# Two-layer hybrid trunk: in the RWKV pairs, the value mix behind the 16x16 inverse, the bonus sum in the eighth PSUM bank, the removal-query transposes behind the key-query products

## The chip, the cores and the metric

The kernel runs on one core of one Trainium2 chip. The metric is the device time of one execution, in microseconds (us). A core has a matrix engine (TensorE, PE in the profile; its weight loads are PEld), a vector engine (VectorE, DVE), an activation engine (ScalarE, ACT), GpSimd (POOL) and SyncE (SP). Here nearly all transfers are issued from SP's queue, in the order of the program. Matrix products are written to PSUM, which has eight banks of 128x512 fp32; this kernel gives them out as four kinds of buffer: `bank` (tag a, two), `bank2` (tag b, two), `gbank` (tag g, three) and `bank3` (tag h, one, "the eighth bank").

## The reference, cut to what matters

Each of the two layers normalises x (512 tokens, 2048 features), multiplies it with a wide input matrix, runs three branches (mLSTM, latent attention, RWKV-7), gates and joins their outputs and multiplies with an output matrix. The branch that the change touches:

```python
def rwkv7_branch(rw_mix, v_first, vres, mu, w0, w2, a0, a2, k_k, k_a, r_k, ln_g, ln_b):
    xm = rw_mix.astype(jnp.float32)
    xs = xm + mu * (token_shift(xm) - xm)
    r, k, v, xw, xa = jnp.split(xs, [...], axis=-1)
    decay = jnp.exp(-jnp.exp(-jax.nn.softplus(-(w0 + jnp.tanh(xw) @ w2)) - 0.5))
    a = jax.nn.sigmoid(a0 + xa @ a2)
    if vres is None:                      # layer 0
        v_first = v
    else:                                 # layer 1: the value mix
        v0, v1, v2 = vres
        v = v + (v_first - v) * jax.nn.sigmoid(v0 + (v @ v1) @ v2)
    kk = heads(k * k_k)                   # 8 heads of 64
    kk = kk / jnp.maximum(jnp.sqrt(jnp.sum(kk * kk, axis=-1, keepdims=True)), 1e-12)
    k_h = heads(k * (1.0 + (a - 1.0) * k_a))
    y = rwkv7_scan(heads(r), heads(decay), k_h, heads(v), -kk, kk * heads(a))
    y = head_layer_norm(y, ...)           # then the bonus:
    y = y + jnp.sum(heads(r) * k_h * r_k, axis=-1, keepdims=True) * heads(v)
    return y.reshape(B, T, RW_WIDTH), v_first
```

The scan is S = S*w + (S a) b^T + v k^T, y = S r, over 512 tokens. `a_vec` = -kk is the removal query, `b_vec` = kk*a the removal key.

## The kernel before, in words

Matrix products with full precision are done in three passes: an operand is split in a rounded part and a rest (`hi`, `lo`), ACT makes the first and DVE the second (L150, L151 for weights; L252, L254 in `split2`).

Per layer, the input product is cut in 26 blocks of 256 columns. `gemm` (L221) makes a generator of 8 steps for each block; each step is 12 matmuls of 128x512 (24 of 128x256 for `mv`) in PSUM tiles called `pg0_..` and `pg1_..`. The weights come in pieces of 512 KB (`raw_..`) from SP's queue, two buffers deep. The generators stand in one list, `bg`. The foreground work, which has long chains of small operations, calls for them: `bg.along(ratio, main, side)` runs a foreground generator and takes `ratio` background steps for each of its `yield`s; `bg.ensure(name)` runs background steps until the block `name` is done. So where the code yields, and where it needs a block, sets how much of the input product is written beside which foreground work. From that order of the code a list scheduler with a timing model (`schedule_with_timeline_sim=True`) makes a fixed order for each engine when the program is built; on the chip each engine takes its instructions in that order. Inside `with in_order():` PE's order is as written.

The foreground of a layer, in order: four pairs of RWKV heads (`rw_pair`, L694, ratio 1.0); then `rw_states` beside the mLSTM heads 0 and 1 (`ml_head`, ratio 0.8); then three short preparations of the attention beside the mLSTM heads 2 and 3; then `bg.ensure("az3")`, the last of the input product; then the attention (`attention`, ratio 0.0), and the output product (`po`, L1390).

A pair works on two heads, that is 128 features by 512 tokens, in 8 chunks of 64 tokens. Its chain: decays `E`, `Ei` and gate `al`; keys `k` and their norm (`psn`, a product with block ones that sums over a head); `ar` holds the removal queries and the queries, `bk` the two kinds of keys (four POOL instructions, L785); the bonus sum (`psbo`, `head_sum` at L760) is copied to `bv`; the values `v` are fetched, in layer 1 mixed with layer 0's (L767 to L776: a product `psv2`, a sigmoid, three DVE instructions and a fetch of `vf`), multiplied into the bonus and parked; values and removal queries are transposed to token-major form (`psTv` to `UV`, `psTa` to `AR`; `token_major`, L790). Then the key-query products of each chunk (`psG`, 16 matmuls in two `bank` and two `bank2` tiles) go masked to `GG` (L822), and the keys are transposed (`psTk`). The 16x16 diagonal blocks go through DRAM (`inv_d`) to a layout in which DVE inverts them in a loop of short instructions (`TX`, L879 to L890), and back (`tx`); two doublings to 64x64 follow (`psQ`, `psT32`, `psQ64`, `psX64`). `psQ` stands in one in-order stretch with `psR` (L919), the first product that reads `UV`. The products with the inverse (`psW`, `psM`, `psN`, `psY`) end the pair.

`fetch("rv")` (L764) asks for the block `rv0` or `rv1` of the values, and in layer 1 line 766 asks for `rv1` in any case, so in the first pair of a layer the code there runs all background steps up to that block.

Of the kernel before, what the change touches and what calls it, by code (L numbers as in the profile page):

```python
# [12 lines left out]
F32 = mybir.dt.float32  # L13
# [4 lines left out]
ALU = mybir.AluOpType  # L18
# [40 lines left out]
R_MU, R_W0, R_A0, R_KK, R_KA, R_RK, R_LG, R_LB, R_V0 = 66, 79, 83, 87, 91, 95, 99, 103, 107  # L59
# [14 lines left out]
def trunk(ctx, tc, a, out):  # L74
    nc = tc.nc
    mm = nc.tensor.matmul
# [3 lines left out]
    tt = nc.vector.tensor_tensor  # L80
    dma = nc.sync.dma_start

    def in_order():

        return tc.manual_schedule(engines={mybir.EngineType.PE})
# [10 lines left out]
    def bank(name):  # L96
        return psb.tile([128, 512], F32, tag="a", bufs=2, name=name)
# [121 lines left out]
    bg = Work()  # L219
# [31 lines left out]
    def split2(hi, lo, src, scale=1.0):  # L251
        act(hi, src, AF.Copy, scale=scale)  # L252
        if isinstance(scale, float) and scale == 1.0:
            tt(lo, src, hi.bitcast(F32), ALU.subtract)  # L254
        else:
            stt(lo, src, scale, hi.bitcast(F32), ALU.mult, ALU.subtract)

    def sigm(dst, src, hbias):

        act(dst, src, AF.Tanh, scale=0.5, bias=hbias)  # L260
        tsc(dst, dst, 0.5, 0.5, ALU.mult, ALU.add)
# [112 lines left out]
    ps = bank("psng")  # L374
# [140 lines left out]
    vf_d = dram.tile([4, 128, T], F32, name="vf_d")  # L515

    for l in range(DEPTH):
        bg.done.clear()

        def pc(r, l=l):  # L520
            return prm[l][:, r:r + 1]

        def pch(r, l=l):
            return prh[l][:, r:r + 1]
# [8 lines left out]
        kept = {}  # L533
# [137 lines left out]
        tail_d = dram.tile([4, 3, 128, T], F32, name=f"tail_d{l}")  # L671
        xp = xp_ctx.enter_context(tc.tile_pool(name=f"xp{l}", bufs=1, side="left"))
        rp = rp_ctx.enter_context(tc.tile_pool(name=f"rp{l}", bufs=1, side="right"))
# [9 lines left out]
        if l > 0:  # L683
            v1 = rp.tile([128, 4, 32], F32, name=f"v1_{l}")
            nc.gpsimd.dma_start(v1, a["rw_v1"][l - 1].rearrange("(k p) r -> p k r", p=128))
            raw = rp.tile([32, T], F32, tag="UV", name=f"v2r_{l}")
            nc.gpsimd.dma_start(raw, a["rw_v2"][l - 1])
            v2 = rp.tile([128, T], F32R, name=f"v2_{l}")
# [5 lines left out]
        def rw_pair(p, l=l):  # L694
            nm = f"{l}_{p}"

            def tmp(name):
                return rp.tile([128, T], F32, tag="tmp", bufs=4, name=f"{name}{nm}")
            whh, ahh, wl, al_ = kept["wa"]

            def fetch(kind):
                bg.ensure(f"{kind}{p // 2}")
                t = rp.tile([128, T], F32, tag=f"x{kind}", name=f"x{kind}{nm}")
                dma(t, vf_d[p] if kind == "rv" and l == 0 else park_d[PARK[kind] + p])
                return t
            inv_d = inv_ds[p]

            def head_sum(x, tag, name):

                hl = rp.tile([128, 2, T], F32R, tag=tag, name=f"{name}x{nm}")  # L710
                split2(hl[:, 0], hl[:, 1], x)
                ps = bank(f"{name}{nm}")
                for u in range(2):
                    mm(ps, lhsT=bones, rhs=hl[:, u], start=(u == 0), stop=(u == 1))
                return ps
            sl = slice(p * 128, (p + 1) * 128)

            ps = bank(f"psw{nm}")
# [6 lines left out]
            s = tmp("s")  # L725
# [14 lines left out]
            act(inv, k, AF.Square, scale=pc(R_KK + p))  # L740
            ps = head_sum(inv, "UV", "psn")
            yield
# [6 lines left out]
            ar = rp.tile([128, 2, 8, 64], F32, tag="ar", name=f"ar{nm}")  # L749
# [7 lines left out]
            tt(kk, kk, al, ALU.mult)  # L757
            bo = tmp("bo")
            stt(bo, r, pc(R_RK + p), kh, ALU.mult, ALU.mult)
            ps = head_sum(bo, "AR", "psbo")  # L760
            yield
            bv = tmp("bv")
            nc.scalar.copy(bv, ps)
            v = fetch("rv")  # L764
            if l > 0:
                bg.ensure("rv1")
                ps = bank(f"psv2_{nm}")  # L767
                mm(ps, lhsT=v2[:, p * 128:(p + 1) * 128], rhs=kept["vv"], start=True, stop=True)
                yield
                s = tmp("vs")  # L770
                sigm(s, ps, pch(R_V0 + p))
                vf = tmp("vf")
                dma(vf, vf_d[p])
                tt(vf, vf, v, ALU.subtract)
                tt(vf, vf, s, ALU.mult)
                tt(v, v, vf, ALU.add)  # L776
            tt(bv, bv, v, ALU.mult)
            dma(tail_d[p, 0], bv)

            hs = [slice(0, 64), slice(64, 128)]  # L780
            bk = rp.tile([128, 8, 2, 64], F32, tag="bk", name=f"bk{nm}")
# [8 lines left out]
            def token_major(blocks, dst, nn, bank_=bank):  # L790

                ps = bank_(f"psT{nn}{nm}")
                for tb in range(4):
                    nc.tensor.transpose(ps[:, tb * 128:(tb + 1) * 128], blocks(tb), idf)
                pv = ps.rearrange("p (a n) -> p a n", n=128)
                for par in range(2):
                    for h in range(2):
                        o, i_ = dst(h).rearrange("p (a b) n -> p a b n", b=2)[:, :, par, :], pv[hs[par], :, hs[h]]
                        if h == par:
                            nc.scalar.copy(o, i_)  # L800
                        else:
                            nc.vector.tensor_copy(o, i_)

            UV = rp.tile([128, 2, 8, 64], F32, tag="UV", name=f"UV{nm}")
            token_major(lambda tb: v[:, tb * 128:(tb + 1) * 128], lambda h: UV[hs[1 - h], h], "v")
            AR = rp.tile([128, 8, 128], F32, tag="AR", name=f"AR{nm}")
            token_major(lambda tb: ar[:, 0, 2 * tb:2 * tb + 2, :].rearrange("p c n -> p (c n)"),
                        lambda h: AR[hs[h], :, 0:64], "a", bank2)
            yield
            yield  # L810

# [3 lines left out]
            with in_order():  # L815
                for c in range(8):
                    for h in (1, 0):
                        mm(pv[c // 4][h][:, c % 4, :], lhsT=bk[hs[h], c].rearrange("p s t -> p (s t)"),
                           rhs=ar[hs[h], :, c, :], start=True, stop=True)
# [6 lines left out]
            for half in range(2):  # L826
                ps = bank(f"psTk{half}{nm}")
                for c in range(4):
                    nc.tensor.transpose(ps[:, c * 128:c * 128 + 128],
                                        bk[:, half * 4 + c].rearrange("p s t -> p (s t)"), idf)  # L830
                (nc.scalar.copy, nc.vector.tensor_copy)[half](
                    GG[:, :, half * 4:half * 4 + 4, 128:192], ps.rearrange("p (c h n) -> p h c n", h=2, n=64))
            yield
            def cross(n, lhs, rhs, name, banks_):


                pv = [b_(f"{name}{odd}{nm}")[:, 0:4 * n].rearrange("p (c n) -> p c n", n=n)
                      for odd, b_ in enumerate(banks_)]
                for c in range(0, 8, 2):
                    for odd in (1, 0):  # L840
                        for h in (1, 0):
                            mm(pv[odd][hs[h ^ odd], c // 2, :], lhsT=lhs(h, c + odd), rhs=rhs(h, c + odd),
                               start=True, stop=True)
                return pv
# [56 lines left out]
            def flip():  # L901

                nc.vector.transpose(X32.rearrange("p c t -> p (c t)"), T32.rearrange("p c t -> p (c t)"))
            flip()
            for _ in range(3):
                yield

            def prod32(lhs, rhs, name):
# [7 lines left out]
            def blk(m):  # L916
                return lambda q, c, e=0: m[q, c, :]
            Q = small([128, 8, 32], "Q", "Qa")
            with in_order():  # L919
                psQ = prod32(lambda q, c, n: GG[q, n // 2, c, n % 2 * 32:n % 2 * 32 + 32], blk(T32), "psQ")  # L920
                psR = cross(64, lambda h, c: GG[hs[1 - h], h, c, 0:64], lambda h, c: UV[hs[1 - h], h, c, :], "psR",
                            (bank2, bank2))
            tt(Q, psQ, mq.rearrange("p a b -> p (a b)")[:, None, :].broadcast_to([128, 8, 32]), ALU.mult)
            nc.scalar.copy(AR[:, 0:8:2, 64:128], psR[0])
            nc.scalar.copy(AR[hs[0], 1:8:2, 64:128], psR[1][hs[1]])
            nc.vector.tensor_copy(AR[hs[1], 1:8:2, 64:128], psR[1][hs[0]])
            yield
# [7 lines left out]
            ps = bank(f"psQ64{nm}")  # L935
            pv = ps[:, 0:256].rearrange("p (c n) -> p c n", n=32)
            Q = small([128, 8, 32], "Q", "Qb")
            for c in range(8):
                for h in range(2):
                    mm(pv[q4[2 * h + 1], c, :], lhsT=GG[q4[2 * h], h, c, 32:64], rhs=T32[q4[2 * h], c, :],  # L940
                       start=True, stop=True)
# [3 lines left out]
            ps = bank(f"psX64{nm}")  # L945
            pv = ps[:, 0:256].rearrange("p (c n) -> p c n", n=32)
            for c in range(8):
                for h in (1, 0):
                    mm(pv[q4[2 * h], c, :], lhsT=Q[q4[2 * h + 1], c, :], rhs=X32[q4[2 * h + 1], c, :],
                       start=True, stop=True)  # L950
# [6 lines left out]
            with in_order():  # L957
                W = cross(128, lambda h, c: X[hs[h], c, :], lambda h, c: AR[hs[h], c, :], "psW", (bank, bank2))
            even, odd = slice(0, 8, 2), slice(1, 8, 2)
            nc.scalar.copy(UV[hs[0], 0, odd, :], W[1][hs[1], :, 64:128])  # L960
            nc.vector.tensor_copy(UV[hs[1], 1, odd, :], W[1][hs[0], :, 64:128])
            nc.scalar.copy(Wm[hs[0], odd, :], W[1][hs[1], :, 0:64])
# [178 lines left out]
        for p in range(4):  # L1141
            bg.along(R_PAIRS, rw_pair(p))
# [398 lines left out]
```

## Time and profile before

| | us |
|---|---|
| median of 3 runs | 1999.47 (1997.14 to 2000.08) |
| the profiled execution | 2003.1 |
| span of that execution, first to last instruction | 2001.4 |
| PE busy in the span | 1953.5 (98%) |
| DVE busy | 1234.5 (62%) |
| ACT busy | 861.5 (43%) |
| POOL busy | 136.2 (7%) |
| mean share of the full TensorE clock granted | 0.991 |

Busy time is a sum over the whole span, with work of many stages in it; a wait in one stage can only be read from that stage. A matmul of 128x512 stands in the profile with about 390 ns, since its end is modelled; the next one starts about 227 ns after it, and that is the pace by which stretches of them are added up. The trace shows layer 0's input product until about 699 us and its attention until 825 us; layer 1's until 1674 and 1827 us. Before each, the rows give what ended an engine's idle time, as far as semaphores tell.

### The profile page before, as it was taken

The page shows a single profiled execution, that of the slowest core. Times are in us where ns is not written, and L with a number is a line of the kernel's source. Part 1 is how long each engine was busy: PE and PEld are TensorE (multiplying, and loading weights), DVE is VectorE, ACT ScalarE, POOL GpSimd, SP SyncE. Part 2 cuts the span into 40 slices and gives each one's busy share as a digit, 9 for nine tenths or more (in the row PEclk, how much of TensorE's full clock was granted, in tenths as well). Part 3 has the DMA queues.
Part 4 walks back from the last instruction along what each step waited for, and adds up shares of the span by engine and source line. Part 5 has one row for each costly group of instructions (what it writes and reads, how often), then busy time and mean ns, then how long its engine had stood idle before and what let it go on. Part 6 is the DMA issues. An engine that isn't in the chain of part 4 may idle for free.

```text
span 2001.4 us, 31675 instructions
## 1 busy us (share of the span) xinstructions
PE 1953.5 (98%) x12544; PEld 1622.1 (81%) x12544; DVE 1234.5 (62%) x2115; ACT 861.5 (43%) x1483; POOL 136.2 (7%) x168
## 2 busy tenths in 40 slices
PE   8999999999999999999999999999999998799998
PEld 6888888888888878888887788888888877687886
DVE  6864867575666499533365458567664768785343
ACT  6534343434546355323353234242423566554233
POOL 4010101100000021000001001010100001110000
PEclk9999999999999999999999999999999999899999
DMA  5443434335555443344444443434345555233334
GB/s 175 136 132 115 121 117 127 111 106 169 162 177 173 124 118 122 101 137 135 144 116 135 127 111 117 127 117 132 109 121 163 169 172 168 76 121 122 116 116 158
DMA packets 246393, 264.86 MB, mean 132 GB/s; under 512 B 49972, under 2 KB 178174, under 8 KB 246246
## 3 DMA queue, kind: packets, MB, share of 16 engines
q1 hardware_dynamic: 245398, 261.88, 42.9%
q8 instruction: 98, 1.61, 0.3%
q0 software_dynamic: 848, 0.97, 0.2%
q14 instruction: 49, 0.40, 0.1%
HBM read 212.45 MB, written 50.35 MB: 131 GB/s over the span
## 4 chain that ended last, share of the span: by engine, by line
PE 87%; DVE 6%; DMA 2%; issue 2%; ACT 2%; SPq 0%; ACTq 0%; DVEq 0%
PE po L1390 17%; PE pg_az L239 7%; PE pg_rr L239 4%; PE pg_mo L239 4%; PE pg_rz L239 4%; PE pg_rk L239 4%; PE pg_rv L239 4%; PE pg_mz L239 4%; PE pg_cq L239 4%; PE pg_mv L235 4%; PE pg_mq L239 3%; PE pg_mk L239 3%; PE pssc L1311 2%; PE pg_ck L239 2%; PE pg_misc L239 2%
## 5 line engine op out<-in xcount | busy, mean ns | idle before, releaser
L1390 PE MATMUL po<-whi_o,mh 128*128 128x512 f32 x512 | 200.3, 391 | 0.1
L1390 PE MATMUL po<-whi_o,ml 128*128 128x512 f32 x512 | 199.4, 389 | 0.0
L151 DVE TENSOR_TENSOR wlo_o<-raw_o,whi_o 128x1024 fp32r<-128x1024 f32 x64 | 78.3, 1224 | 188.4 <-ACT whi_o L150 187.3
L1390 PE MATMUL po<-wlo_o,mh 128*128 128x512 f32 x512 | 187.8, 390 | 0.0
L150 ACT ACTIVATE whi_o<-raw_o 128x1024 fp32r<-128x1024 f32 x64 | 67.7, 1059 | 204.6 <-PE po L1390 166.3
L1390 PEld LDWEIGHTS po<-whi_o,mh 128*128 128x128 f32 x512 | 96.1, 188 | 20.5 <-DVE Vl L254 0.6
L1390 PEld LDWEIGHTS po<-wlo_o,mh 128*128 128x128 f32 x512 | 96.1, 188 | 19.9
L1390 PEld LDWEIGHTS po<-whi_o,ml 128*128 128x128 f32 x512 | 96.1, 188 | 19.6
L239 PE MATMUL pg_az<-xh,whi_az 128*128 128x512 f32 x256 | 101.5, 397 | 0.0
L239 PE MATMUL pg_az<-xl,whi_az 128*128 128x512 f32 x256 | 100.9, 394 | 0.0
L239 PE MATMUL pg_az<-xh,wlo_az 128*128 128x512 f32 x256 | 100.0, 396 | 0.0
L235 PE MATMUL pg_mv<-wlo_mv,xh 128*128 128x256 f32 x256 | 73.2, 286 | 1.4 <-DVE wlo_mv L151 1.4
L235 PE MATMUL pg_mv<-whi_mv,xl 128*128 128x256 f32 x256 | 72.9, 285 | 0.0
L235 PE MATMUL pg_mv<-whi_mv,xh 128*128 128x256 f32 x256 | 72.6, 284 | 0.0
L785 POOL TENSOR_TENSOR bk<-kk,Ei 64x512 f32<-64x512 f32 x16 | 27.5, 1717 | 443.3 <-DVE E L730 230.6
L239 PEld LDWEIGHTS pg_az<-xh,wlo_az 128*128 128x128 f32 x256 | 48.5, 190 | 9.7
L239 PEld LDWEIGHTS pg_az<-xh,whi_az 128*128 128x128 f32 x256 | 48.6, 190 | 9.6
L239 PEld LDWEIGHTS pg_az<-xl,whi_az 128*128 128x128 f32 x256 | 48.6, 190 | 9.5
L151 DVE TENSOR_TENSOR wlo_az<-raw_az,whi_az 128x1024 fp32r<-128x1024 f32 x32 | 39.1, 1222 | 20.6 <-ACT whi_az L150 20.3
L239 PE MATMUL pg_rk<-xl,whi_rk 128*128 128x512 f32 x128 | 51.6, 404 | 0.0
L239 PE MATMUL pg_rk<-xh,whi_rk 128*128 128x512 f32 x128 | 51.0, 402 | 0.5 <-ACT xh L252 0.5
L239 PE MATMUL pg_cq<-xh,whi_cq 128*128 128x512 f32 x128 | 51.2, 400 | 0.0
(572 smaller groups left out, 5548.9 us busy)
## 6 DMA issues: line engine op xcount, KB each, us to landing
raw_o<-in_w_out_dram SPq DMA_DIRECT2D x64, 512.0 KB
raw_az<-in_w_in_dram SPq DMA_DIRECT2D x32, 512.0 KB
raw_rk<-in_w_in_dram SPq DMA_DIRECT2D x16, 512.0 KB
raw_rr<-in_w_in_dram SPq DMA_DIRECT2D x16, 512.0 KB
raw_rv<-in_w_in_dram SPq DMA_DIRECT2D x16, 512.0 KB
raw_rz<-in_w_in_dram SPq DMA_DIRECT2D x16, 512.0 KB
raw_mq<-in_w_in_dram SPq DMA_DIRECT2D x16, 512.0 KB
raw_mk<-in_w_in_dram SPq DMA_DIRECT2D x16, 512.0 KB
```

Source lines behind the costliest of these rows:

```text
L150: act(hi, raw, AF.Copy)
L151: (nc.gpsimd if name[0] == "u" or name in ("misc0_0", "misc0_1") else nc.vector).tensor_tensor(lo, raw, hi.bitcast(F32), ALU.subtract)
L235: mm(ps[u][:, (tb % 2) * 256:(tb % 2) * 256 + 256], lhsT=xx[:, sl], rhs=w[:, i, :], start=(k == 0 and n == 0 and tb % 2 == 0), stop=(k == ...
L239: mm(ps[u], lhsT=w[:, i, u * 128:(u + 1) * 128], rhs=xx, start=(k == 0 and n == 0), stop=(k == 15 and n == 2))
L785: nc.gpsimd.tensor_tensor(bk[q, :, slot, :], x[q].rearrange(c64, t=64), Ei[q].rearrange(c64, t=64), ALU.mult)
L1311: mm(ps[:, 0:n], lhsT=x1[:, ts_], rhs=x2[:, 0:n], start=(j == 0), stop=(j == 5))
L1390: mm(pss[tb], lhsT=xx[:, sl], rhs=w, start=(k == korder[0] and j == 0), stop=(k == korder[15] and j == 2))
```

## The change

Three blocks of `rw_pair` are moved or change their bank. The bonus sum takes `bank3` instead of `bank`. Fetch and mix of the values, the product with the bonus, the store of `bv` and the transposes to `UV` move from ahead of `psG` to behind the inverse's last instruction `flip()`; one of the three `yield`s that stood there is now ahead of the block. The transposes of the removal queries to `AR` move from ahead of `psG` to behind `psTk`. The number of `yield`s of a pair is the same. No instruction of PE, DVE, POOL or SP is added or removed; ACT has six table loads fewer.

```diff
-            def head_sum(x, tag, name):
+            def head_sum(x, tag, name, bank_=bank):
...
-                ps = bank(f"{name}{nm}")
+                ps = bank_(f"{name}{nm}")
...
-            ps = head_sum(bo, "AR", "psbo")
+            ps = head_sum(bo, "AR", "psbo", bank3)
             yield
             bv = tmp("bv")
             nc.scalar.copy(bv, ps)
-            v = fetch("rv")
-            if l > 0:
...
-            tt(bv, bv, v, ALU.mult)
-            dma(tail_d[p, 0], bv)
...
-            UV = rp.tile([128, 2, 8, 64], F32, tag="UV", name=f"UV{nm}")
-            token_major(lambda tb: v[:, tb * 128:(tb + 1) * 128], lambda h: UV[hs[1 - h], h], "v")
-            AR = rp.tile([128, 8, 128], F32, tag="AR", name=f"AR{nm}")
-            token_major(lambda tb: ar[:, 0, 2 * tb:2 * tb + 2, :].rearrange("p c n -> p (c n)"),
-                        lambda h: AR[hs[h], :, 0:64], "a", bank2)
             yield
             yield
...
+            AR = rp.tile([128, 8, 128], F32, tag="AR", name=f"AR{nm}")
+            token_major(lambda tb: ar[:, 0, 2 * tb:2 * tb + 2, :].rearrange("p c n -> p (c n)"),
+                        lambda h: AR[hs[h], :, 0:64], "a", bank2)
             yield
...
             flip()
-            for _ in range(3):
+            yield
+            v = fetch("rv")
+            if l > 0:
+                bg.ensure("rv1")
+                ps = bank(f"psv2_{nm}")
+                mm(ps, lhsT=v2[:, p * 128:(p + 1) * 128], rhs=kept["vv"], start=True, stop=True)
+                yield
+                s = tmp("vs")
+                sigm(s, ps, pch(R_V0 + p))
+                vf = tmp("vf")
+                dma(vf, vf_d[p])
+                tt(vf, vf, v, ALU.subtract)
+                tt(vf, vf, s, ALU.mult)
+                tt(v, v, vf, ALU.add)
+            tt(bv, bv, v, ALU.mult)
+            dma(tail_d[p, 0], bv)
+
+            UV = rp.tile([128, 2, 8, 64], F32, tag="UV", name=f"UV{nm}")
+            token_major(lambda tb: v[:, tb * 128:(tb + 1) * 128], lambda h: UV[hs[1 - h], h], "v")
+            for _ in range(2):
                 yield
```

What the scheduler makes of it is seen at three places. Names end in layer, pair or head, and a buffer number; `psbo1_1` is layer 1, pair 1. The first place is PE in pair 1 of layer 1, from the bonus sum to the key-query products. Before:

```order
L714 MATMUL psbo1_1_10999<-psbox1_1_10996,bones_435 128x512
L768 MATMUL psv2_1_1_11026<-vv1_10329,v2_1_9582 128x512
L235 MATMUL pg0_mv01_11940<-whi_mv01_0_11857,xh1_0_8276 128x256
...
L714 MATMUL psbo1_1_10999<-psbox1_1_10996,bones_435 128x512
...
L235 MATMUL pg1_mv01_11941<-whi_mv01_1_11944,xl1_5_8297 128x256
L794 MATMUL psTv1_1_11058<-idf_87,xrv1_1_11024 128x128 x4
L818 MATMUL psG011_1_11108<-ar1_1_10985,bk1_1_11050 128x128
```

Now:

```order
L714 MATMUL psbo1_1_10915<-psbox1_1_10912,bones_435 128x512
L239 MATMUL pg0_mq01_11417<-xh1_12_8288,whi_mq01_3_11603 128x512
...
L797 MATMUL psG011_1_10970<-ar1_1_10901,bk1_1_10932 128x128
L797 MATMUL psG001_1_10969<-ar1_1_10901,bk1_1_10932 128x128
...
L808 MATMUL psTk11_1_11026<-idf_87,bk1_1_10932 128x128 x4
...
L779 MATMUL psTa1_1_11033<-idf_87,ar1_1_10901 128x128 x4
...
L893 MATMUL psv2_1_1_11117<-vv1_10420,v2_1_9582 128x512
...
L779 MATMUL psTv1_1_11142<-idf_87,xrv1_1_11115 128x128 x4
```

Between the last matmul of `psbo` and the first of `psG` stood 73 matmuls of the input product; now 8 stand there, and the value product and both transposes come behind `psTk`.

The second place is DVE in the same pair, in the loop of the 16x16 inverse. Before:

```order
L862 TENSOR_REDUCE dg1_1_11178<-wide1_1_11056 128x128
L151 TENSOR_TENSOR wlo_mo01_0_12271<-raw_mo01_0_12166,whi_mo01_0_12270 128x1024
L879 TENSOR_TENSOR TX1_1_11183<-A161_1_11181,TX1_1_11183 64x2
L880 TENSOR_REDUCE TX1_1_11183<-TX1_1_11183 64x2
L879 TENSOR_TENSOR TX1_1_11183<-A161_1_11181,TX1_1_11183 64x8
L880 TENSOR_REDUCE TX1_1_11183<-TX1_1_11183 64x2x2
L879 TENSOR_TENSOR TX1_1_11183<-A161_1_11181,TX1_1_11183 64x18
```

Now:

```order
L862 TENSOR_TENSOR TX1_1_11067<-A161_1_11065,TX1_1_11067 64x2
L261 TENSOR_SCALAR vs1_1_11131<-vs1_1_11131 128x512
L863 TENSOR_REDUCE TX1_1_11067<-TX1_1_11067 64x2
L899 TENSOR_TENSOR vf1_1_11134<-vf1_1_11134,xrv1_1_11115 128x512
L862 TENSOR_TENSOR TX1_1_11067<-A161_1_11065,TX1_1_11067 64x8
L266 SCALAR_TENSOR_TENSOR sg_nmq1_0_11659<-sg_nmq1_0_11659,sg_mq1_0_11658 128x512
L900 TENSOR_TENSOR vf1_1_11134<-vf1_1_11134,vs1_1_11131 128x512
L863 TENSOR_REDUCE TX1_1_11067<-TX1_1_11067 64x2x2
L901 TENSOR_TENSOR xrv1_1_11115<-xrv1_1_11115,vf1_1_11134 128x512
```

The steps of the value mix (`vs`, `vf`, `xrv`) stand between the steps of the inverse; before, they stood ahead of the masks `GG`.

The third place is PE at the end of layer 1's input product (`az3`), where the attention begins with `psqr`. `psSm1_3` and `psHT1_3` are products and transposes of mLSTM head 3. Before:

```order
L239 MATMUL pg1_az31_15726<-xh1_15_8291,wlo_az31_3_15791 128x512
L1248 MATMUL psqr1_0_15868<-cqh1_0_14934,whi_uqr1_0_15821 128x512
...
L1130 MATMUL psHT1_2_15162<-idf_87,hn1_2_15157 128x128
L1203 MATMUL psrcq1_15055<-ones_92,cqr3_1_15049 128x1 x4
...
L1085 MATMUL psSm1_3_0_15202<-mqh1_3_15176,mkh1_3_15178 128x512
...
L1130 MATMUL psHT1_3_15307<-idf_87,hn1_3_15302 128x128 x4
L1248 MATMUL pskn1_2_16130<-ckh1_0_14942,whi_uqk1_2_15972 128x512
```

Now:

```order
L1087 MATMUL psSm1_3_3_15268<-mqh1_3_15176,mkl1_3_15179 128x512
...
L1132 MATMUL psHT1_3_15307<-idf_87,hn1_3_15302 128x128 x3
L239 MATMUL pg0_az21_15591<-xh1_10_8286,wlo_az21_2_15626 128x512
...
L239 MATMUL pg1_az31_15726<-xl1_15_8307,whi_az31_3_15790 128x512
L239 MATMUL pg1_az31_15726<-xh1_15_8291,wlo_az31_3_15791 128x512
L1250 MATMUL psqr1_0_15868<-cqh1_0_14934,whi_uqr1_0_15821 128x512
```

Head 3 stood wholly behind the last matmul of the input product; now 134 matmuls of it stand behind head 3's last transpose. Counted at the end of layer 1's pairs (the last `psY` of pair 3), 494 matmuls of the input product were left before, 712 now; in layer 0 838 and 910.

## Rows read from the trace of the kernel before

**Rows 1.** The page, part 1: busy time, share of the span, instructions.
```profile
PE 1953.5 (98%) x12544; PEld 1622.1 (81%) x12544; DVE 1234.5 (62%) x2115; ACT 861.5 (43%) x1483; POOL 136.2 (7%) x168
```
**Rows 2.** Stretches: us, busy us per engine (x instructions), PEclk, DMA share, GB/s.
```profile
665.00:775.00 110.00, 106.79 (x566) 90.01 (x566) 81.32 (x166) 54.88 (x117) 22.69 (x14) 0.98 0.40 115
1640.00:1750.00 110.00, 90.07 (x464) 73.88 (x463) 84.78 (x181) 68.98 (x143) 16.78 (x10) 0.89 0.41 125
1640.00:1650.00 10.00, 7.04 (x33) 5.81 (x32) 6.57 (x11) 7.12 (x11) 0.00 (x0) 0.72 0.39 134
1710.00:1720.00 10.00, 2.12 (x9) 1.20 (x8) 3.98 (x14) 4.01 (x12) 0.00 (x0) 0.63 0.15 52
```
**Rows 3.** Waits of PE, 1600 us to the end: us in total, times, longest.
```profile
PE pskn L1248 <- DVE Vl L254: 4.4, 1, 4.4
PE psHT L1130 <- DVE hn L1126: 3.6, 1, 3.6
PE psv L1276 <- DVE qrf L1221: 2.4, 1, 2.4
```
**Rows 4.** Timeline of PE, first and last matmul of each layer's attention: start, us.
```profile
698.63 0.39 PE L1248 MATMUL psqr<-cqh,whi_uqr 128*128 128x512 f32 x1
824.39 0.27 PE L1352 MATMUL pso<-PTh,Vl 128*128 128x128 f32 x1
...
1673.44 0.39 PE L1248 MATMUL psqr<-cqh,whi_uqr 128*128 128x512 f32 x1
1826.65 0.27 PE L1352 MATMUL pso<-PTh,Vl 128*128 128x128 f32 x1
```
**Rows 5.** Chain that ended last, pieces: start us, us, what.
```profile
669.75 27.02 PE pg_az L239 x119
1583.45 0.53 PE psSm L1085 x3
1707.09 1.42 PE psN L1099 x13
449.34 3.30 PE pg_mv L235 x26
1602.20 4.51 DMA nb<-row_d
```
**Rows 6.** Timeline of PE, layer 1, pair 1: bonus sum to `psQ`.
```profile
1240.99 0.39 PE L714 MATMUL psbo<-psbox,bones 128*128 128x512 f32 x1
1249.98 0.60 PE L794 MATMUL psTv<-idf,xrv 128*128 128x128 f32 x4
1250.51 0.48 PE L818 MATMUL psG<-ar,bk 64*128 64x128 f32 x2
1255.06 2.05 PE L818 MATMUL psG<-ar,bk 64*128 64x128 f32 x30
1281.11 0.67 PE L913 MATMUL psQ<-T,GG 32*32 32x32 f32 x56
```
**Rows 7.** Waits of PE, 200 to 500 us.
```profile
PE psT L913 <- DVE Qa L923: 2.1, 2, 1.1
PE pg_mv L235 <- DVE wlo_mv L151: 1.4, 2, 0.9
PE psQ L913 <- DVE T L898: 0.4, 1, 0.4
```
**Rows 8.** Tiles `vf`, `UV`, `bk`: ns min/median/max, first and last start.
```profile
L774 DVE TENSOR_TENSOR vf<-vf,xrv x4: 676/680/691, 1133.6 to 1452.6; 128x512 f32<-128x512 f32 x4
L802 DVE COPY UV<-psTv x16: 404/422/429, 121.6 to 1460.4; 64x256 f32<-64x256 f32 x16
L785 POOL TENSOR_TENSOR bk<-kk,Ei x16: 1580/1617/2176, 98.2 to 1443.2; 64x512 f32<-64x512 f32 x16
```
**Rows 9.** Timeline, layer 1, pair 1: last matmul of `psn` (PE), last of `bk` (POOL).
```profile
1220.71 0.39 PE L714 MATMUL psn<-psnx,bones 128*128 128x512 f32 x1
1235.85 3.85 POOL L785 TENSOR_TENSOR bk<-kh,Ei 64x512 f32<-64x512 f32 x2
```

More of the change, by code (lines that the diff above doesn't have):

```diff
@@ L763, in rw_pair @@
             nc.scalar.copy(bv, ps)
-            v = fetch("rv")
-            if l > 0:
[L766 to L776, printed above, removed]
-            tt(bv, bv, v, ALU.mult)
-            dma(tail_d[p, 0], bv)
             hs = [slice(0, 64), slice(64, 128)]
```

## The prediction

> **What bounds the kernel now.** The page's busy times come first: PE is busy 98% of the span, DVE 62%, ACT 43% [rows 1]. PE's work is the same before and after, so the change can win only PE's idle time and the time in which its clock was low, and lose only by new waits of PE. The busy times over stretches say where there is anything to win: in the 110 us around the start of layer 1's attention (1640 to 1750 us) PE is idle for 110 - 90.07 = 19.9 us, in the like stretch of layer 0 (665 to 775 us) for 3.2 us; the granted clock is 0.89 in the one and 0.98 in the other [rows 2]. The waits of PE there end with DVE: with the rest of the values (`Vl`) for the key product, with `hn` for the transposes of an mLSTM head, with `qrf` of the rope [rows 3]. In the pairs of RWKV heads PE hardly waits: the three largest waits from 200 to 500 us sum to 3.9 us [rows 7].
>
> Why layer 1 idles there and layer 0 does not stands in the order of PE: in layer 1 the whole mLSTM head 3 comes behind the last matmul of the input product, so its chain of DVE, ACT and PE steps has nothing big beside it and competes with the attention's start. In layer 0 the head is done before.
>
> **The change part by part.** The number of `yield`s is the same. What changes is the length of a pair's chain. In pair 1 of layer 1 the last matmul of the bonus sum started at 1240.99 us, `psTv` at 1249.98, the first of `psG` at 1250.51 and its last 30 at 1255.06 [rows 6]: 9.5 us from bonus sum to key-query products, filled by 73 matmuls of the input product. Now 8 stand there. In the first pair of layer 1 it was 241 of them, because the value mix asked for block `rv1`; now none. So the pairs of layer 1 are written with less of the input product beside them, and 712 instead of 494 of its matmuls are left when the pairs end: 218 more, at 27.02/119 = 0.227 us [rows 5] some 49 us of filler that moves behind the pairs. It now lies beside the mLSTM heads: 134 matmuls, 30 us, stand behind head 3's last transpose, where there was none. That is layer 0's picture, and the two layers do the same work, so layer 0 gives the price.
>
> First term, the attention's stretch. From the first `psqr` to the end of the last `pso` layer 0 takes 824.66 - 698.63 = 126.0 us, layer 1 takes 1826.92 - 1673.44 = 153.5 us [rows 4], 27.5 us more. Of these, work that layer 1 had to do inside: 30 matmuls `psN` at 1.42/13 = 0.109 us, 3.3 us; 12 `psSm`, 3 x (512 + 384 + 256 + 128) columns at 0.53/3 us for 384 [rows 5], 1.8 us; eight transposes and the small `psrcq`, by the pace of `psN` about 1.8 us. Sum 6.9 us, which moves and isn't saved. Lost: 20.6 us.
>
> Second term, 1640 to 1650 us, ahead of that stretch: PE idle 10 - 7.04 = 3.0 us, and a granted clock of 0.72, that is 5.6 us at the lower of its two levels (1.2 instead of 2.4 GHz) [rows 2], half of them lost where PE worked, about 2 us. The two terms give 25.6 us.
>
> The same counted the other way: idle 19.9 - 3.2 = 16.7 us; time at 1.2 GHz 2 x 0.11 x 110 = 24 us against 2 x 0.02 x 110 = 4 us, so 20 us less of it. If PE had worked through all of that, 10 us would come back; but in 1710 to 1720 us, at a mean clock of 0.63, it was idle for 7.9 of 10 us [rows 2], so I take 6 us. Sum 22.7 us. I take 24 us, between the two counts.
>
> The granted clock fell after PE had sat idle. Here a page of the Trainium skill can be weighed: TensorE: Matmul & The Clock Gate, section Terms, puts the penalty of a throttled stretch at its length times the share of the clock withheld, half. By it the 20 us would give back 10 us, and the sum would be 26.7 us; the row of 1710 to 1720 us speaks for less, since an idle engine loses nothing.
>
> Third term, the waits inside the pairs. The 3.9 us of layer 0 [rows 7] can go or grow. From `psG` to `psQ` pair 1 of layer 1 took 1281.11 - 1257.11 = 24.0 us [rows 6] without a wait of PE, with 58 matmuls of 512 and 82 of 256 columns between (58 x 0.227 + 82 x 0.127 = 23.6 us). Now DVE has more to do there. In layer 1: the mix, three of 0.68 us and the sigmoid's end, the product with the bonus, 0.68 us, and two copies each for `UV` and `AR` at 0.42 us [rows 8], near 4.9 us; in layer 0 without the mix, 2.4 us. PE has more there too: in layer 1's pairs 1 to 3 32.2, 29.7 and 29.1 us of the input product by the same paces (before 23.6, 27.9 and 23.6), in pair 0 56 us; in layer 0 25.2, 26.8, 23.4 and 26.6 us (before 25.7, 22.9, 23.4 and 26.6). So layer 1 is covered, and pairs 0, 2 and 3 of layer 0 may lack up to 2.4 us each. Bounds: -4 us (all waits gone) and +7 us from layer 0; I take +0.5 us, since a scheduler with the same timing model left 3.9 us in these chains before.
>
> At nothing I cost: the bonus sum's bank (no other tile of the pairs uses it), the store of `bv` and the fetches on SP, which wait there as before between loads of weights that run two ahead (PE's wait for a weight split was 1.4 us in all [rows 7], and that is the price scale if this cover fails), six ACT table loads less (ACT is 43% busy), and layer 0's 72 matmuls moved behind its pairs, where PE already had filler.
>
> Sum: 24 - 0.5 = 23.5 us less. The profiled execution took 2003.1 us, 3.6 us above the median of the runs, 1999.47; I take the saving from the median: **1976 us**.
>
> **Rivals.**
>
> *The wait moves along.* The heads' chain is late for reasons that filler doesn't cure: loads of 4.51 us like `nb` [rows 5] and DVE, busy 84.8 of 110 us [rows 2]. Then PE meets half of the 24 us where head 2 and 3 now stand: 1988 us. For it: PE's waits name DVE [rows 3]. Against: layer 0 runs the same heads beside the input product and idles 3.2 us in 110.
>
> *The waits of the pairs go as well.* With the shorter chain to `psG` and the larger of the two counts: 25.6 + 4 = 30 us, 1970 us.
>
> *The change doesn't do what it says.* `psG` now stands where the keys `bk` have just been made, and POOL would hold it. In pair 1 of layer 1, `bk` was done at 1239.70 us, 18.6 us after the end of the last `psn` at 1221.10 [rows 9]; PE now has 91 matmuls, 20.7 us, of the input product from `psn` to `psG`, 2.1 us to spare, the least of the eight pairs. The four instructions of `bk` take between 1.58 and 2.18 us each [rows 8]; with all at the upper end a pair would lose 2.2 us over the median, just what is spare. If no pair had slack, 8 x 2.2 = 18 us would come back: 1994 us. On this the Trainium skill has a rule that speaks against the change (SBUF — State Buffer, section SBUF: two separate sides): GpSimd shares a port pair with VectorE, and either blocks the other for a whole instruction when VectorE reads two tensors from SBUF. The spread of `bk` agrees with it.
>
> *Slower.* The value steps stand between the steps of the inverse on DVE, and `vf` comes from DRAM at that point. If the mix waits for its load, every later step of `TX` waits behind it, and PE, whose order is fixed, stands at `psQ`. Price: a load of 4.51 us [rows 5] in each of four pairs, 18 us, and all added DVE work uncovered, 4 x 4.9 + 4 x 2.4 = 29 us: 47 us, 23 us above the saving, 2023 us. It decides from 24 us of new waits, 3 us a pair. Against: the filler ahead of `psQ` grew by 1.8 to 8.6 us in layer 1's pairs 1 to 3.
>
> **How the numbers follow.** Forecast, 1970 to 1982 us: 0.70. The wait moves along, 1982 to 1995: 0.13. The pairs' waits go too, below 1970: 0.06. POOL holds `psG`, around 1994: 0.04. Slower: 0.05; 0.02 is left for no change at all. A difference under 0.2% (4 us) can't be told from none here. Faster therefore 0.90, same 0.04, slower 0.06. The range 1967 to 1988 us leaves out the worse half of the first rival, POOL and the slower case.
>
> **What would show it.** Right: from layer 1's first `psqr` to its last `pso` 126 to 130 us instead of 153.5; a granted clock near 0.98 there; no wait of PE for `hn`; the last `psY` of layer 1 about 49 us earlier; `psG` within 2 us of the bonus sum; PE's waits in the pairs below 8 us. Wrong: PE idle at `psQ` or `psR` for more than 3 us a pair, idle at `psSm` or `psN` beside the input product, or layer 1's attention still above 140 us.

## The result and the profile after

The changed kernel takes 1973.26 us (median of 4 runs, 1971.44 to 1973.56), beside 1999.78 us (4 runs, 1997.14 to 2002.26) for the kernel before on the same chip: a ratio of 0.9866, 95% interval 0.9849 to 0.9883. The forecast was 1976 us.

The profiled execution took 1973.39 us with a span of 1971.7 us, 29.7 us less than the span before. The page's busy times, as in [rows 1]:

```profile
PE 1939.3 (98%) x12544; PEld 1614.6 (82%) x12544; DVE 1223.6 (62%) x2115; ACT 854.4 (43%) x1477; POOL 135.1 (7%) x168
```

The four stretches of [rows 2], same columns (the fourth number, after the length, is PE's busy time; the one after the engines is the granted clock):

```profile
665.00:775.00 110.00, 106.77 (x578) 90.39 (x577) 81.18 (x175) 57.70 (x125) 22.98 (x14) 0.98 0.37 107
1640.00:1750.00 110.00, 106.76 (x567) 90.00 (x566) 80.27 (x168) 54.84 (x118) 23.14 (x14) 0.98 0.39 113
1640.00:1650.00 10.00, 10.00 (x48) 8.25 (x47) 4.90 (x6) 3.09 (x4) 0.00 (x0) 1.00 0.47 138
1710.00:1720.00 10.00, 9.82 (x59) 8.13 (x60) 9.58 (x30) 7.04 (x21) 1.29 (x1) 1.00 0.24 73
```

Layer 1's start of the attention has become layer 0's: 106.76 us busy in place of 90.07, a clock of 0.98 in place of 0.89. First and last matmul of each layer's attention, as in [rows 4]:

```profile
692.77 0.39 PE L1250 MATMUL psqr<-cqh,whi_uqr 128*128 128x512 f32 x1
...
819.37 0.28 PE L1354 MATMUL pso<-PTh,Vl 128*128 128x128 f32 x1
...
1671.63 0.39 PE L1250 MATMUL psqr<-cqh,whi_uqr 128*128 128x512 f32 x1
...
1797.15 0.27 PE L1354 MATMUL pso<-PTh,Vl 128*128 128x128 f32 x1
```

The attention takes 126.9 us in layer 0 (126.0 before) and 125.8 us in layer 1 (153.5 before). PE's waits from 1600 us to the end, the longest two, where [rows 3] had `Vl` with 4.4 and `hn` with 3.6 us (columns: us in total, times, longest):

```profile
PE psv L1278 <- DVE qrf L1223: 2.6, 1, 2.6
PE pssc L1313 <- ACT pp L1318: 1.2, 2, 0.6
```

And from 200 to 500 us, where [rows 7] had 3.9 us:

```profile
PE psT L915 <- issue: 1.0, 1, 1.0
PE psSm L1087 <- ACT mkh L252: 0.4, 1, 0.4
PE psT L915 <- DVE Qa L925: 0.2, 1, 0.2
```

Pair 1 of layer 1 on PE, as in [rows 6]:

```profile
1207.07 0.40 PE L714 MATMUL psbo<-psbox,bones 128*128 128x512 f32 x1
...
1207.98 0.40 PE L714 MATMUL psbo<-psbox,bones 128*128 128x512 f32 x1
...
1210.12 2.06 PE L797 MATMUL psG<-ar,bk 64*128 64x128 f32 x32
...
1246.22 0.75 PE L915 MATMUL psQ<-T,GG 32*32 32x32 f32 x64
```

`psG` comes 2.1 us after the bonus sum (9.5 us before) and takes 2.1 us in one piece (6.6 us before, in two).

The span's 29.7 us, by these rows: layer 1's attention 27.7 less, of which 6.9 are head 3's own work, which moved ahead of it, so 20.8 us; the stretch from layer 0's last `pso` to layer 1's first `psqr` grew from 848.8 to 852.0 us, 3.2 us in place of those 6.9, so 3.7 us less; layer 0 up to its first `psqr` 5.9 us less; layer 0's attention 0.9 us more; the end 0.2 us less. The 6.9 us are the prediction's count; in the changed kernel the same products of head 3 take 6.6 us from start to next start, so 0.3 us may belong to the first of these terms instead of the second. The spans differ by 3.2 us more than the medians (26.5 us), since the profiled execution of the kernel before took 2003.1 us, 3.3 us above its median; the terms are known no better than that.

### The profile page after: what moved, and what is told of

The parts are those of the page before. It is cut to its first block, busy times and chain, and to the rows that moved or that the text cites. A ratio compares the mean times of both kernels' runs of the same rounds, so it can differ in the third digit from the quotient of the medians.

```text
span 1971.7 us, 31648 instructions
## 1 busy us (share of the span) xinstructions
PE 1939.3 (98%) x12544; PEld 1614.6 (82%) x12544; DVE 1223.6 (62%) x2115; ACT 854.4 (43%) x1477; POOL 135.1 (7%) x168
## 4 chain that ended last, share of the span: by engine, by line
PE 89%; DVE 5%; ACT 2%; DMA 2%; issue 1%; SPq 0%; ACTq 0%; DVEq 0%
PE po L1392 18%; PE pg_az L239 8%; PE pg_rk L239 5%; PE pg_mq L239 5%; PE pg_rz L239 5%; PE pg_rr L239 4%; PE pg_rv L239 4%; PE pg_mo L239 4%; PE pg_mv L235 4%; PE pg_mk L239 4%; PE pg_cq L239 4%; PE pg_mz L239 4%; PE pg_ck L239 2%; PE pg_misc L239 2%; PE pssc L1313 2%
## 5 line engine op out<-in xcount | busy, mean ns | idle before, releaser
L150 ACT ACTIVATE whi_az<-raw_az 128x1024 fp32r<-128x1024 f32 x32 | 33.8, 1055 | 49.8 <-PE pg_az L239 35.7
```

The source lines that it names most:

```text
L150: act(hi, raw, AF.Copy)
```

## The experiments

Theory A was the prediction's: what counts is how many matmuls of layer 1's input product (0.227 us each, [rows 5]) are left for the mLSTM heads, above all behind head 3's last transpose `psHT`. The rival was that the pairs themselves are time: fewer steps and waits in their chains. Every run was timed over five rounds beside the kernel before, whose medians in the three sessions were 2001.6, 2002.42 and 2002.08 us (the second session, with the kernel without the mix and the small parts, values with queries and values with bank, was on another chip, so kernels of different sessions are compared by their ratios). The table has the span's stages from the traces, in us: the end of layer 0's last `pso`; from there to layer 1's last `psY`; from there to layer 1's first `psqr` counted from the same point; layer 1's attention; and the matmuls behind head 3.

| kernel | median | ratio (95%) | layer 0 ends | to last `psY` | to `psqr` | attention | left |
|---|---|---|---|---|---|---|---|
| before | | 1 | 824.7 | 699.2 | 848.8 | 153.5 | 0 |
| changed | 1973.26 | 0.9866 (0.9849 to 0.9883) | 819.6 | 651.2 | 852.0 | 125.8 | 134 |
| layer 1 only | 1978.4 | 0.9887 (0.9872 to 0.9902) | 824.4 | 652.3 | 852.3 | 126.1 | 134 |
| layer 0 only | 1997.67 | 0.9979 (0.997 to 0.9987) | 820.7 | 699.9 | 848.7 | 153.2 | 0 |
| values only | 1985.62 | 0.9923 (0.9911 to 0.9936) | 824.6 | 657.7 | 859.1 | 125.8 | 120 |
| cover taken away | 2003.11 | 1.0009 (1.0 to 1.0018) | 819.5 | 651.2 | 844.0 | 163.0 | 0 |
| no value mix | 1982.53 | 0.9901 (0.9888 to 0.9915) | 825.2 | 655.9 | 856.2 | 125.8 | 134 |
| small parts | 1994.9 | 0.9966 (0.9952 to 0.9979) | 821.9 | 700.7 | 845.6 | 151.2 | 0 |
| values, queries | 1978.55 | 0.9882 (0.9869 to 0.9896) | 824.2 | 655.2 | 853.9 | 125.8 | 96 |
| values, bank | 1982.62 | 0.9902 (0.9888 to 0.9915) | 825.6 | 656.0 | 856.6 | 125.7 | 120 |
| more on DVE | 1982.74 | 0.9902 (0.9885 to 0.9918) | 824.6 | 662.1 | 855.3 | 127.4 | 54 |

**Layer 1 only** and **layer 0 only**: the kernel before, with all three parts under `if l > 0:`, or under `if l == 0:`.

```diff
-            ps = head_sum(bo, "AR", "psbo")
+            ps = head_sum(bo, "AR", "psbo", bank3 if l > 0 else bank)
...
-            v = fetch("rv")
+            if not (l > 0):
+                v = fetch("rv")
```

> All three edits in layer 1 alone; layer 0 as before. 712 matmuls of layer 1's input product are left when its pairs end and 134 behind mLSTM head 3, as in the changed kernel. Theory A (filler moved behind layer 1's pairs covers head 3 and the attention's start): nearly the whole gain, 20 to 24 us off, about 1977 to 1980 us; layer 1's first psqr to last pso 126 us. Theory B (shorter chains and fewer waits in the pairs of both layers): half the gain, about 1987 us.

> All three edits in layer 0 alone; layer 1 as before, with nothing of the input product left behind head 3. Theory A: layer 0's tail was covered already, so only its waits in the pairs change, 3 to 6 us off, 1994 to 1997 us; layer 1's attention stretch stays at 153 us. Theory B: half the gain, about 1987 us.

Measured 23.2 and 3.9 us below the kernel before's 2001.6. Both as theory A had it: the attention falls to 126.1 us in the one and stays at 153.2 us in the other. The two gains sum to 27.1 us; both layers together gave 26.8, by the ratio.

**Cover taken away**: the changed kernel, with the rest of the input product ordered ahead of mLSTM heads 2 and 3 in layer 1.

```diff
+        if l > 0:
+            bg.ensure("az3")
```

> The changed kernel, with the rest of layer 1's input product written ahead of mLSTM heads 2 and 3 (the ensure of its last block moved ahead of them): 712 matmuls are still left at the pairs' end, but none behind heads 2 and 3. Theory A: the gain in layer 1 is lost or more, 20 to 30 us slower than the changed kernel, 1994 to 2003 us; layer 1's attention stretch, with the heads in it, above 145 us. Theory B (the gain arises in the pairs): stays near 1973 us, at most 5 us slower.

The pairs are as short as in the changed kernel (651.2 us to the last `psY`), and the whole gain is gone: 2003.11 us, 0.1 us above the upper end of theory A's range. Layer 0 keeps its 5 us; layer 1, from layer 0's end to the end of its attention, takes 1007.0 us, against 977.8 in the changed kernel and 1002.3 in the kernel before. So this run takes away somewhat more cover than the change gave: head 2's last transpose comes 27 us behind `psqr`, in the kernel before 4 us. Of PE's waits from 1500 to 1760 us the first two are those of [rows 3]:

```profile
PE pskn L1250 <- DVE Vl L254: 4.3, 1, 4.3
PE psHT L1132 <- DVE hn L1128: 3.6, 1, 3.6
PE psqn L1250 <- DVE knl L254: 3.1, 1, 3.1
```

So in layer 1 the shorter pairs gain nothing by themselves; they are worth what they leave over for the heads.

**No value mix**: the kernel before, in which layer 1 leaves out `psv2`, its sigmoid, the load of `vf` and the three vector operations; nothing is moved.

```diff
-            if l > 0:
-                bg.ensure("rv1")
...
-                tt(v, v, vf, ALU.add)
```

> The kernel before, in which layer 1 leaves out the value mix (the product psv2, its sigmoid, the load of vf and three vector operations per pair): its values are then not mixed with layer 0's. Nothing is moved. Theory A (the time lies in the matmuls of the input product that are left for the heads): the program leaves 134 of them behind head 3's last norm instead of 0, so layer 1's attention takes 125 to 128 us instead of 153.5, and the whole 1976 to 1986 us. Rival (what the move saves are the waits that stood in the pairs, of which the trace before shows 0.9 us in layer 1): little can go but PE's four products, 0.4 us each, so 1998 to 2001 us.

As theory A: leaving the mix out frees 134 matmuls as moving it does, and the attention falls to 125.8 us. The rival's 1998 us is out.

**Values only**: neither the bank nor the removal queries changed.

```diff
-            v = fetch("rv")
...
+            yield
+            v = fetch("rv")
```

> Only the values move; the bonus sum stays in its old bank and the removal queries are transposed ahead of the key-query products. 694 matmuls are left when layer 1's pairs end, 120 behind head 3. Theory A: 22 to 27 us off, within 3 us of the changed kernel, 1973 to 1977 us. Rival (the bank and the transposes matter, since psG waits for its banks and for AR): a third or more of the gain is missing, 1982 us or above.

This one missed: 1985.62 us is outside theory A's range and in the rival's. The attention is whole (125.8 us), yet the run stands 11.4 us above the changed kernel by the ratios, 2000 x (0.9923 - 0.9866). The trace has the loss in two places: 5.0 us in layer 0, and 7.1 us from layer 0's end to layer 1's `psqr`. Of the latter, PE's waits above 0.1 us are 1.9 us more, and 6.83 us at the lower clock cost about 3.3 us: the 20 matmuls that start in them take 6.77 us from start to next start, 3.3 us more than the medians of the same kinds at the upper clock. The other 1.9 us weren't traced. Wait and lower clock stand in one place. The stretch 1550 to 1562 us, first of the kernel with the values alone, then of the changed kernel:

```profile
1550.00:1562.00 12.00, 10.08 (x66) 8.58 (x65) 8.48 (x20) 7.58 (x18) 0.00 (x0) 0.72 0.51 158
```

```profile
1550.00:1562.00 12.00, 12.00 (x82) 9.94 (x81) 8.10 (x12) 5.75 (x9) 0.00 (x0) 1.00 0.70 222
```

And what PE waited for in the kernel with the values alone (start, us, engine; in brackets the idle time before and what ended it):

```profile
1551.37 1.04 ACT L150 ACTIVATE whi_ck<-raw_ck 128x1024 fp32r<-128x1024 f32 x1
...
1552.44 1.23 DVE L151 TENSOR_TENSOR wlo_ck<-raw_ck,whi_ck 128x1024 fp32r<-128x1024 f32 x1 [1.04 <-ACT whi_ck L150]
1553.58 0.42 DVE L1094 SCALAR_TENSOR_TENSOR me<-psSm,me 128x256 f32<-128x256 f32 x1
...
1554.03 0.42 ACT L252 ACTIVATE meh<-me 128x256 fp32r<-128x256 f32 x1 [1.43 <-DVE me L1094]
...
1554.50 0.48 PE L1101 MATMUL psN<-mvh,meh 128*128 128x130 f32 x1 [1.92 <-ACT meh L252]
```

Behind it the matmuls of the input product start 0.43 us apart, and then 0.24 us:

```profile
1559.18 0.63 PE L239 MATMUL pg_ck<-xl,whi_ck 128*128 128x512 f32 x1
1559.61 0.63 PE L239 MATMUL pg_ck<-xh,wlo_ck 128*128 128x512 f32 x1
...
1561.50 0.40 PE L239 MATMUL pg_ck<-xl,whi_ck 128*128 128x512 f32 x1
1561.74 0.39 PE L239 MATMUL pg_ck<-xh,wlo_ck 128*128 128x512 f32 x1
```

DVE stands 1.04 us before a weight split that is first in its fixed order and 1.23 us in it, while the head's mask step `me`, on which PE waits, is queued behind. The kernel with values and bank has the same wait (2.0 us at `psN`, and 3.41 us at the lower clock), the one with values and queries has not: the wait goes with the order that the scheduler makes around it.

**Small parts**, **values and queries**, **values and bank**: the other three combinations.

```diff
-            ps = head_sum(bo, "AR", "psbo")
+            ps = head_sum(bo, "AR", "psbo", bank3)
```

(in the first and the third; the block of `AR` behind `psTk` in the first and the second; the values moved in the second and the third.)

> The two small parts without the large one: bonus sum in the eighth bank and removal queries transposed behind the key-query products; the values stay where they were. Theory A: 0 matmuls of the layer's input product are left behind head 3 in layer 1 (42 behind head 2), as before, so layer 1 gains nothing beyond a few us; layer 0 gains the 4 us of the run with the change in layer 0 alone; 1993 to 1999 us. Rival (the two parts are worth the 12 us by which the run with the values alone stood above the changed kernel, wherever the values are): 1988 to 1991 us.

> The changed kernel with the bonus sum back in the first banks: values and removal queries moved. 96 matmuls of the input product are left behind head 3 in layer 1 (134 in the changed kernel, 120 with the values alone). Theory A: the large term is kept, 1972 to 1986 us. Within it, if the 12 us missing with the values alone belong to the transposes that stood ahead of psG, 1972 to 1977 us; if they belong to the bank of the bonus sum, 1982 to 1986 us. Rival (cover must be 134 to be whole): at 38 matmuls less, each 0.23 us, 8.7 us more than the changed kernel, so 1982 us.

> The changed kernel with the removal queries' transposes back ahead of psG: values and bonus sum moved. 120 matmuls are left behind head 3 in layer 1, as with the values alone. Theory A: the large term is kept, 1972 to 1986 us. Within it, if the 12 us missing with the values alone belong to the transposes, 1982 to 1986 us; if to the bank, 1972 to 1977 us. If they were a chance wait at the heads (the run with the values alone shows 1.92 us at a psN at 1552.6 us and 6.83 us at the lower clock behind it, 5.3 us together), about 1978 us whenever that wait is not met.

The small parts alone: attention 151.2 us, nothing left behind head 3, 6.8 us off, in the range of theory A. Its waits from 1500 to 1760 us still begin as before:

```profile
PE pskn L1249 <- DVE Vl L254: 4.3, 1, 4.3
PE psqn L1249 <- DVE knl L254: 2.2, 1, 2.2
PE psqn L1249 <- ACT whi_uqk L150: 2.0, 1, 2.0
```

The rival's 1988 to 1991 us for the small parts is out. With the values moved, the queries take 8 us more off and the bank 4 us, by the ratios; together 11.4. (Each ratio is uncertain by 2.5 to 3.5 us either way.) The expectation for the values with the bank named about 1978 us where the chance wait at the heads isn't met: the kernel with the queries doesn't meet it and took 1978.55 us, the one with the bank meets it and took 1982.62 us. The hypothesis that 134 matmuls are needed is out: 96 serve as well (attention 125.8 us), and 54 (below) nearly (127.4 us).

Layer 0 ends early (819.1 to 821.9 us) only in kernels that have both small parts there; with one of them, or none, it ends at 824.2 to 825.6 us. With the values moved, `psG` takes 2.0 to 2.1 us in layer 0's pairs 1 to 3 where both small parts are there, and 6.1 to 7.0 us where one or both are missing. The code says why it should take both: `psG` writes two `bank` and two `bank2` tiles, all there are of each, and the bonus sum in its old bank holds one of the first, the queries' transposes ahead of it one of the second. But in the kernel before it takes 2.1 to 3.1 us there, and layer 0 ends at 824.7 us all the same, so `psG` alone doesn't explain it.

What goes with layer 0's end better is the prediction's own measure, the matmuls of the input product left when its pairs end, counted in the traces: 910 left, and it ends at 819.1 to 820.7 us; 871 left, 821.9 to 824.6 us; 832 to 838 left, 824.4 to 825.6 us.

**More on DVE**: the changed kernel with six products more per pair, whose result is not used.

```diff
+            pad = tmp("pad")
+            for _ in range(6):
+                tt(pad, v, v, ALU.mult)
```

> The changed kernel with six more VectorE products of 128x512 (0.68 us each, so 4.1 us in each of eight pairs, 33 us in all) in every pair's inverse, behind the bonus product; what they make is not used. Theory A (a pair's chain may grow at no cost as long as matmuls of the input product are left for the heads): the program still leaves 54 of them behind head 3 in layer 1 (134 in the changed kernel) and 128 in layer 0, so layer 1's attention stays at 126 us, and the whole is 1972 to 1980 us. Rival (the chain on VectorE is time, the price of the prediction's slower case): 33 us more, 2000 to 2006 us.

Above theory A's range and far under the rival's: the 33 us added cost 7.2 us by the ratios, 10.3 us between the two spans. Layer 0's pairs did grow by nearly all of it (its last `psY` at 464.5 instead of 450.0 us, for 16.4 us added), layer 1's by 10.9 us of 16.4, and the matmuls left over paid for most. What came through in the trace is 5.0 us in layer 0, 3.3 us ahead of layer 1's `psqr` and 1.6 us in its attention. Layer 0 is the telling part: both small parts are there, but only 836 matmuls are left at its pairs' end instead of 910, and it ends as late (824.6 us) as in the kernel before (838 left). Both have a wait of PE at `psN` of a head near 530 us, and the lower clock near its end (3.41 us in the kernel before, 6.83 us in this one); first the kernel before:

```profile
PE psN L1099 <- DVE mvl L254: 1.2, 1, 1.2
```

```profile
PE psN L1104 <- ACT meh L252: 1.9, 1, 1.9
```

The changed kernel has neither there, but a wait of 1.0 us for `hn`. The waits behind the rest weren't taken apart.

**Attention's first steps changed over**: two orders for the first steps of the attention of the changed kernel, aimed at the 2.58 us that PE waits at the first `psv` in each layer.

```diff
-    yield from (("rope", 0), ("in", 0), ("v", 0))
+    yield from (("in", 0), ("rope", 0), ("v", 0))
```

```diff
-    yield from (("rope", 0), ("in", 0), ("v", 0))
+    yield from (("in", 0), ("v", 0), ("rope", 0))
```

> The changed kernel with the first two steps of each layer's attention changed over: head 0's key and query products ahead of the first pair's rotation. In the changed kernel TensorE waits 2.58 us at the first psv in each layer for qrf on VectorE, and 3.41 us at the lower clock follow, 4.3 us per layer together. Theory A: with psqr behind psqn and pskn its bank is asked for again later, but the banks of psqn and pskn must then be read first, so a shorter wait stands in its place; 0 to 8.6 us less, 1965 to 1973 us. Rival (the wait only moves to the next bank): 1971 to 1974 us.

> The changed kernel with the first pair's rotation put behind head 0's products and the first values. Theory A, as for the kernel with the first two steps changed over: 0 to 8.6 us less, 1965 to 1973 us; here the rotation is needed by the first scores right behind it, which then wait for five VectorE operations of 0.7 us, so a wait at pssc of up to 4 us per layer would take the place of the one at psv: 1971 to 1976 us. Rival (only the wait's length matters, wherever it stands): as the other order.

1972.94 us (ratio 0.9854, 0.984 to 0.9869) and 1973.66 us (0.9858, 0.9844 to 0.9873): neither can be told from the changed kernel. The first one's longest waits from 1500 to 1760 us:

```profile
PE psv L1278 <- DVE qrf L1223: 1.1, 1, 1.1
PE psqn L1250 <- DVE qrf L1223: 0.9, 1, 0.9
PE pssc L1313 <- ACT knh L252: 0.6, 1, 0.6
PE pskn L1250 <- DVE qnl L254: 0.5, 1, 0.5
```

One wait of 2.6 us has become several, of which these four sum to 3.1 us; the clock stayed at its upper level there, and that gained nothing either. The times lie in the ranges of both theories, so they don't decide; the rows speak for the rival (the wait moves to the next bank).

## Why the prediction was right, and where it was off

- *First term, layer 1's attention takes layer 0's time:* 27.5 us between the layers in the kernel before, 27.7 us gone from layer 1; without head 3's own work 20.6 us forecast and 20.8 measured. The mechanism is shown from three sides: the cover taken away brings the loss back with the short pairs still there, leaving the mix out brings the attention's gain (125.8 us) without the move, and the small parts alone leave the attention at 151.2 us.
- *The chain's 49 us of filler:* layer 1's last `psY` came 48.0 us earlier counted from layer 0's end.
- *Second term, 1640 to 1650 us:* forecast 5.0 us, measured with all else ahead of layer 1's attention 3.7 us. The stretch itself is full now (10.00 of 10 at clock 1.00). By these two terms the larger of the two counts, 25.6, was the better one (24.5 measured), and I took 24.
- *Third term, the pairs' waits:* the step that failed in sign. I took a loss of 0.5 us; layer 0 up to its first `psqr` gave 5.9 us back, and the run with layer 0 alone 3.9 us in the median. I had bounded a gain at the 3.9 us of PE's waits in [rows 7]. Of the 5.9 us, PE's waits above 0.1 us are 2.0, of which 1.2 is the wait at `psN` near 530 us, behind the pairs. The other 3.9 are busy time of PE (686.1 to 682.2 us): from start to next start, waits taken off, `psG` went from 9.2 to 7.9 us, `psN` from 17.3 to 16.2 us, the input product's matmuls by 1.5 us. The same products needn't have the same busy time, then, though the prediction's first paragraph let the change win only idle time and low clock.
- *The sum:* 26.5 us between the medians against 23.5 forecast; the 3 us lie about in layer 0's part, 3.9 us gained in the run with layer 0 alone against the 0.5 us of loss.
- *At nothing:* wrong in that bank and queries together are worth 6.8 us without the values and 11.4 with them, by the ratios. I priced the bank as covered and never as part of a chain. Nor was there nothing in layer 0's 72 matmuls that moved behind its pairs: layer 0's end goes with their number, and falls back by 5 us where 836 are left (the run with more on DVE). That is the first term's mechanism in the other layer. It is borne out by that one run and by the order of the others, not by a run that changes the number alone; why 871 left go with 821.9 us in one kernel and 824.2 and 824.6 us in two others stays open.
- *The rivals:* the wait moved along only in part of the kernels with fewer parts (1.92 us at `psN`, above). POOL did not hold `psG`: PE has no wait above 0.1 us at it in the changed kernel. DVE did wait for the load of `vf`, 1.7 us in two of four pairs (before, 0.55 us in one), and PE has no such wait at `psQ` or `psR`.
- *A statement ahead of the prediction* needs mending: that the code's yields and block requests set how much of the input product stands beside a pair. The kernel before and the small parts have as many `yield`s and the same requests, and so have the changed kernel and the one with more on DVE; still 494 and 490, and 712 and 657, matmuls are left when layer 1's pairs end. The lengthened chain of the last one took more of the stock with nothing else changed, so the chain's length counts too.

## What to carry to other kernels

Work that is always ready is a stock that the long chains spend: to find what a shorter chain is worth, count what is left of the stock for the last chain, not the waits inside the shortened one. Check it both ways, with the shortening undone and with the stock spent elsewhere. And where a wait ends with an engine that is busy nearly all the time (here DVE, 12.8 of 15 us, next section), changing the order of the askers may only move the wait, as it did in the two orders tried here.

## What was not expected of the hardware

PE waits 2.57 to 2.59 us at the first `psv` of layer 0 in every kernel with the attention's old order, and of layer 1 in six of those with matmuls left behind head 3 (2.40 us, for another tile, in the seventh, with more on DVE). At 13 of these 17 waits the granted clock fell to its lower level for 3.41 us, at four it did not, among them both of the kernel with values and queries. The 15 us around it, in layer 1 of the changed kernel and then of the other:

```profile
1678.00:1693.00 15.00, 12.42 (x66) 10.85 (x65) 12.81 (x21) 8.77 (x16) 5.61 (x3) 0.89 0.47 143
```

```profile
1684.50:1699.50 15.00, 11.76 (x66) 9.62 (x65) 14.82 (x22) 9.05 (x16) 5.27 (x3) 1.00 0.48 143
```

In the second PE then waits elsewhere (columns as above):

```profile
PE psv L1278 <- DVE qrf L1223: 2.6, 1, 2.6
PE psqn L1250 <- DVE knl L254: 0.7, 1, 0.7
```

Layer 1's attention takes 125.8 us in both, so the lower clock cost nothing that shows there (in layer 0 it takes 125.8 to 126.9 us with it and 125.7 to 126.1 without). DVE is busy 12.8 and 14.8 of the 15 us; the likely reason, which no run isolates, is that the lower clock fell into time in which PE would have waited for DVE. In the kernel with the values alone the 6.83 us at that level fell on a head's products and the input product with no wait between them, and cost 3.3 us. The Trainium skill (TensorE: Matmul & The Clock Gate, section Terms) prices a throttled stretch by its length and the share withheld; the second case agrees (3.4 us by the rule, 3.3 measured), the first, 1.7 us by the rule and none measured in layer 1, does not.
